# A half-swap copied DRAM to DRAM: engines on neighbouring rows, or each engine on 255 rows of its own

## The chip, the cores and the metric

The kernel runs on one core of a Trainium2 chip. Times are device microseconds for one execution on that core. Transfers are carried out by the core's 16 DMA engines; the SP (SyncE) and ACT (ScalarE) queues issue them, and each has a ring of pending transfers on every one of the 16 engines. In the profile, q1 is the ring set of SP and q10 that of ACT.

## The reference

```python
x = np.random.randn(8192, 8192).astype(np.float32)
def reference(x):
    return np.fft.ifftshift(x)
```

For even sizes this exchanges the halves along both axes: `out[r, c] = x[(r + 4096) % 8192, (c + 4096) % 8192]`. Nothing is computed. 8192 x 8192 floats are 268.44 MB, which have to be read once and written once. A row has 32 KB, and a half row, 4096 floats, 16 KB; in a half row source and destination are both contiguous.

## The kernel before

The copy goes from DRAM to DRAM; no tile in on-chip memory is used, and no engine computes. The loop `for row in range(0, R, ENGINES * per)` makes 16 blocks of 512 output rows. For each block, SP issues one transfer for the left half of the rows (`h = 0`) and ACT one for the right half (`h = hc`), 8 MB each, 32 in all.

A transfer is described by three dimensions, each a step and a count, the outermost first. The outermost one has 16 entries, and entry e is carried out by DMA engine e. The second counts the rows that one engine does for this transfer, the third is the contiguous half row of 4096 floats.

```python
per = 32
dims = [[C, ENGINES], [ENGINES * C, per], [1, hc]]
```

With these steps, engine e does rows `row + e`, `row + e + 16`, `row + e + 32` and so on: at any time the 16 engines are at 16 neighbouring rows, and together they go down the block. The packets that the profile counts are half rows of 16 KB; besides them every engine writes one small completion mark for each transfer.

The order of the work is the order of issue. There are four completion semaphores for SP's transfers and four for ACT's, so the fifth transfer of a queue is issued only when the first has landed, the sixth after the second, and so on. An engine alternates between its ring of q1 and its ring of q10 while both hold work. Line 30 of the code holds the transfers, line 48 the start of the program, line 59 its end.

Of the kernel before, what the change touches and what calls it, by code (L numbers as in the profile page):

```python
# [1 line left out]

# [4 lines left out]


ENGINES = 16


@with_exitstack
def kernel(
    ctx: ExitStack,
    tc: tile.TileContext,
    x: bass.AP,
    out: bass.AP,
):
    nc = tc.nc
    R, C = x.shape  # L20
    hr = R // 2
    hc = C // 2


    per = 32
    dims = [[C, ENGINES], [ENGINES * C, per], [1, hc]]
    for row in range(0, R, ENGINES * per):
        src_row = (row + hr) % R
        for queue, h in ((nc.sync, 0), (nc.scalar, hc)):
            queue.dma_start(  # L30
                out=bass.AP(out.tensor, out.offset + row * C + h, dims),
                in_=bass.AP(x.tensor, x.offset + src_row * C + hc - h, dims),
            )


# [1 line left out]
_INS = ['x']  # L37
_OUTS = [((8192, 8192), 'float32')]


def kernel(**inputs):
    import numpy as _np
    import concourse.bacc as _bacc
    import concourse.tile as _tile
    from concourse import mybir as _mybir
    from concourse.bass_utils import run_bass_kernel_spmd as _run

    nc = _bacc.Bacc("TRN2", target_bir_lowering=False, num_devices=1)  # L48
    arrays, args = {}, []
    for name in _INS:  # L50
        a = _np.ascontiguousarray(inputs[name])
        if a.dtype.kind in "iu":
            a = a.astype(_np.int64)
        arrays[f"in_{name}_dram"] = a
        args.append(nc.dram_tensor(f"in_{name}_dram", a.shape, _mybir.dt.from_np(a.dtype), kind="ExternalInput").ap())
    for i, (shape, dtype) in enumerate(_OUTS):
        dt = _mybir.dt.from_np(_np.dtype(dtype))
        args.append(nc.dram_tensor(f"out_{i}_dram", shape, dt, kind="ExternalOutput").ap())
    with _tile.TileContext(nc) as tc:
        kernel(tc, *args)  # L60
    r = _run(nc, [arrays], core_ids=[0])
    got = tuple(r.results[0][f"out_{i}_dram"] for i in range(len(_OUTS)))
    return got[0]
```

## Time and profile before

| what | value |
|---|---|
| median of 3 runs | 822.56 us (821.65 to 823.45) |
| the profiled execution | 822.98 us, span 821.2 us |
| moved | 268.44 MB read, 268.44 MB written |
| mean rate over the span | 327 GB/s in each direction |
| packets | 16,896: 16,384 of 16 KB and 512 completion marks |
| transfers | 16 from SP, 16 from ACT, 8192 KB each |
| issue to landing | median 204 us, shortest 51.6, longest 207.1 |
| computing engines | 0.2 us busy in all (4 constants written by POOL) |

In the profile the line "DMA" gives the mean busy share of the 16 DMA engines in 40 equal slices of the span, in tenths; the line "GB/s" gives what they moved in each slice, counted once (each byte is read once and written once, so the memory sees twice that). In a table of stretches, the columns behind the times are the busy time of computing engines, the clock of TensorE (unused here), the DMA share, and GB/s. In stretches of a microsecond or two the last two columns are coarse, since a packet is counted whole where it starts.

### The profile page before, as it was taken

How to read it: one execution, taken by the hardware profiler on the slowest of the kernel's cores; microseconds unless marked ns; L12 is line 12 of the kernel's file. 1: busy time of each engine (PE TensorE's matmuls, PEld its weight loads, DVE VectorE, ACT ScalarE, POOL GpSimd, SP SyncE). 2: the span in 40 equal slices, each digit the busy share in tenths (PEclk: the TensorE clock that was granted, in tenths of full speed). 3: DMA queues.
4: the chain of work that ended last, by engine and by line, in shares of the span. 5: the costliest groups of instructions: out<-in, count | busy, mean ns of one | idle time of the engine just before them, and what ended most of it. 6: DMA issues, size and time to landing. Idle time of an engine off the chain costs nothing. (4 is left out here: it accounts for less than half of the span.)

```text
span 821.2 us, 77 instructions
## 1 busy us (share of the span) xinstructions
POOL 0.2 (0%) x4
## 2 busy tenths in 40 slices
POOL 0000000000000000000000000000000000000000
DMA  8999999999999999999999999999999999999998
GB/s 296 333 324 329 331 328 334 330 330 329 327 330 329 331 326 332 332 327 328 330 330 330 330 323 330 324 330 330 332 326 329 330 322 333 329 329 327 330 329 276
DMA packets 16896, 268.44 MB, mean 327 GB/s; under 512 B 512, under 2 KB 512, under 8 KB 512
## 3 DMA queue, kind: packets, MB, share of 16 engines
q1 hardware_dynamic: 8448, 134.22, 50.2%
q10 hardware_dynamic: 8448, 134.22, 49.0%
HBM read 268.44 MB, written 268.44 MB: 654 GB/s over the span
## 5 line engine op out<-in xcount | busy, mean ns | idle before, releaser
L48 POOL MEMSET const-bfloat16-1.0<- 128x1 bf16 x1 | 0.1, 102 | 0.0
L48 POOL MEMSET const-uint8-127<- 128x1 uint8 x1 | 0.1, 102 | 0.0
L48 POOL MEMSET const-float32-0.0<- 128x1 f32 x1 | 0.1, 99 | 0.2 <-issue 0.2
L48 POOL MEMSET const-float32-1.0<- 128x1 f32 x1 | 0.1, 99 | 0.0
## 6 DMA issues: line engine op xcount, KB each, us to landing
out_dram<-in_x_dram ACTq DMA_DIRECT2D x16, 8192.0 KB, 204.1
out_dram<-in_x_dram SPq DMA_DIRECT2D x16, 8192.0 KB, 204.0
```

The source lines that it names most:

```text
L48: nc = _bacc.Bacc("TRN2", target_bir_lowering=False, num_devices=1)
```

## The change

The copy, its half rows and the two queues stay. What changes is which rows an engine does, and in which order. The output is taken in two halves of 4096 rows (`base` 0 and 4096). In a half, engine e owns the 255 rows from `base + 255 * e` on, and goes down them one by one. They are cut into five transfers of 51 rows per engine. 16 x 255 are 4080 rows; the 16 rows left over are one more transfer, with one row per engine. So each queue issues 12 transfers instead of 16, and at one time the engines are at rows that lie 255 rows (8,355,840 B) apart instead of one row (32,768 B).

```diff
-    per = 32
-    dims = [[C, ENGINES], [ENGINES * C, per], [1, hc]]
-    for row in range(0, R, ENGINES * per):
+    pitch = 255
+    parts = [51, 51, 51, 51, 51]
+
+    def copy(queue, h, row, pitch, step, n):
+        dims = [[pitch * C, ENGINES], [step * C, n], [1, hc]]
         src_row = (row + hr) % R
-        for queue, h in ((nc.sync, 0), (nc.scalar, hc)):
-            queue.dma_start(
-                out=bass.AP(out.tensor, out.offset + row * C + h, dims),
-                in_=bass.AP(x.tensor, x.offset + src_row * C + hc - h, dims),
-            )
+        queue.dma_start(
+            out=bass.AP(out.tensor, out.offset + row * C + h, dims),
+            in_=bass.AP(x.tensor, x.offset + src_row * C + hc - h, dims),
+        )
+
+    for base in (0, hr):
+        row = base
+        for n in parts:
+            copy(nc.sync, 0, row, pitch, 1, n)
+            copy(nc.scalar, hc, row, pitch, 1, n)
+            row += n
+        rest = base + ENGINES * pitch
+        if rest < base + hr:
+            copy(nc.sync, 0, rest, 1, 1, 1)
+            copy(nc.scalar, hc, rest, 1, 1, 1)
```

## The prediction

> **What bounds the kernel now.** I read the page from the top: the busy table first, then the slices, the DMA queues, the issues with their landings, then the waits of SP's queue and finally stretches of the span.
>
> ```profile
> span 821.2 us, 77 instructions
> POOL 0.2 (0%) x4
> DMA  8999999999999999999999999999999999999998
> GB/s 296 333 324 329 331 328 334 330 330 329 327 330 329 331 326 332 332 327 328 330 330 330 330 323 330 324 330 330 332 326 329 330 322 333 329 329 327 330 329 276
> DMA packets 16896, 268.44 MB, mean 327 GB/s; under 512 B 512, under 2 KB 512, under 8 KB 512
> q1 hardware_dynamic: 8448, 134.22, 50.2%
> q10 hardware_dynamic: 8448, 134.22, 49.0%
> HBM read 268.44 MB, written 268.44 MB: 654 GB/s over the span
> out_dram<-in_x_dram ACTq DMA_DIRECT2D x16, 8192.0 KB, 204.1
> out_dram<-in_x_dram SPq DMA_DIRECT2D x16, 8192.0 KB, 204.0
> ```
>
> No engine computes. The sixteen DMA engines are occupied from the second slice to the last but one, and the 38 whole slices between lie between 322 and 334 GB/s, mean 329.0. Queues q1 and q10 (SP's and ACT's, equal in bytes) share that time: 50.2 + 49.0%. So the time is bytes over pace, and only the pace can change much.
>
> What sets the pace? The trace has 16,384 packets of 16 KB, one for each half row (the other 512 records are the completion marks). The shortest takes 608 ns, about a third take no more than 611 ns, the median is 733, the mean 795 and the 90th percentile 1,092. An engine can therefore do 16,384 B in 608 ns (16 engines: 431 GB/s), and on average is held up for 187 ns by something outside it. Stretches of the span say more:
>
> ```profile
> core 0: us, POOL busy (x), PEclk, DMA share, GB/s
> 2.00:3.00 1.00, 0.00 (x0) 1.00 1.09 262
> 4.00:5.00 1.00, 0.00 (x0) 1.00 1.02 426
> 5.00:6.00 1.00, 0.00 (x0) 1.00 1.03 393
> 10.00:20.00 10.00, 0.00 (x0) 1.00 0.99 318
> 22.00:412.00 390.00, 0.00 (x0) 1.00 1.00 329
> 412.00:802.00 390.00, 0.00 (x0) 1.00 1.00 329
> ```
>
> The engines do come near their own pace once, at 4 to 6 us; from 6 us on they are held to about 329 GB/s, the same in both halves of the output. In stretches of 50 us the rate stays within 326 to 332 GB/s. If the 187 ns were independent bad luck of each packet (their standard deviation is about a quarter of the mean), 50 us with its thousand packets should scatter by 2.7 GB/s; spread evenly over time, the packets' bytes scatter by 1.0. When one packet is slow, others are fast: the engines share a pool, memory traffic of 2 x 329 = 658 GB/s, and the pool is what is full.
>
> ```profile
> SPq L59 <- DMA out_dram<-in_x_dram: 166.8, 2, 119.1
> SPq L30 <- DMA out_dram<-in_x_dram: 134.4, 12, 51.3
> ```
>
> SP waits for landings, not the engines for SP: an issue lands 204 us later, four blocks of 51 us, so the rings hold work throughout.
>
> **The change part by part.** The profiled execution took 822.98 us, 1.78 over its span, and lies 0.42 above the median of 822.56, so the two can be used as one.
>
> *Bytes and packets.* Two times (5 x 51 x 16 + 16) x 2 queues = 16,384 packets of 16 KB, as before. Nothing gained or lost; each engine keeps 1,024 packets.
>
> *Completion marks.* 24 issues instead of 32, so 384 marks instead of 512, 8 fewer per engine at 9 ns each: -0.07 us.
>
> *Issues.* SP and ACT issue 12 each instead of 16. One takes 0.57 to 0.66 us when there is room in the rings, else it stands some 40 us until there is; either way earlier blocks cover it. Issue i waits for issue i-4 of its queue. The thin cover is around the single-row issue: then two blocks of 51 rows and one row are queued, 103 packets per engine and queue. Two queues alternating at 795 ns make that 164 us of work against an issue of 1 us. Without that cover it would cost about an issue, 0.6 to 1.1 us, each time. I put it at 0.
>
> *Start.* SP's first packet starts 2.19 us into the span, 1.5 us after its issue begins, and ACT's first only 2.95 us after SP's. If the delay grows with rows per issue, SP's first issue becomes 0.65 x 51/32 = 1.04 us, +0.4 us; if not, 0. I take +0.2. ACT's later start costs nothing while q1 alone keeps the engines at 426 GB/s.
>
> *End.* The last landings of an issue are spread over 2.6 to 2.9 us across engines, and the last stretch runs dry in that time. The last issue is now one row instead of 32; the engines' shares of the work are equal before and after. 0, bounds -2.9 (they end together) to +3 (as much more).
>
> *The order of addresses*, the only large term. Before, the sixteen engines read 16 neighbouring rows (512 KB) and write 16 neighbouring rows, and go on together. An engine that falls behind by a few packets still touches row residues (modulo 16) that no other engine touches. After, engine i is at row 255 i + t: sixteen streams 8,355,840 B apart on each side. In step, the residues modulo 16 are again all different, (t - i); but an engine one row behind falls on its neighbour's residue, and the sixteen rows are no more one block. Landings of one issue, spread over 2.6 us near the end against 1.6 us for a row's two packets, say that engines are one to two rows out of step. If memory cares for neighbourhood, the change takes some away; I see nothing that it adds, since an engine's two halves of a row, and the 134 MB between read and write row, stay.
>
> The trace holds no row for such a pattern. Bounds: below, packets at their floor, 268.44 MB / 431 GB/s = 623 us of transfer, 4 us of start and end, 627 us; above, every packet as the 90th percentile, x 1,092/795, 816 us x 1.374 + 7 = about 1,128 us. The nearest row for this kernel with a little less order is its own slowest slices, 322 and 323, mean 322.5 against 329.0: 780 us of whole slices become 780.1 x 329.0/322.5 = 795.8, +15.7 us. I take that.
>
> Sum: 822.98 - 0.07 + 0.2 + 15.7 = 838.8, 839 us.
>
> **A rule weighed.** The measured row is this trace's pitch between engines, 32 KB, with 329 GB/s. The Trainium skill ("DMA: Bandwidth & Descriptors", section "Latency and other measured facts", HBM row pitch at large powers of two) reports that copies with rows 8 MiB apart ran at 103 GB/s per direction, and that 4 KiB of padding on a 4 MiB pitch restored 214. The new pitch is 8 MiB less 32 KiB, so by that rule it counts as padded; unpadded, the sum would be 268.44 MB / 103 GB/s = 2,606 us. Its 214 GB/s is already under what this trace shows, so no run here yet tells what a padded pitch allows at 329. The page "HBM Reference", section "Specifications (TRN2)", gives some 716 GB/s for a domain; by it the copy could not go under 536.9 MB / 716 GB/s = 750 us, an estimate.
>
> **The rivals.**
> - *Only the total counts.* For: the evenness over 50 us, and no difference between the halves of the output. Against: a third of the packets run at the floor and others at twice that, so something finer than a total picks them out. Time: 822.98 + 0.1, 823 us.
> - *Neighbouring rows are the cause of the 187 ns* (the other side). Sixteen streams far apart would then collide less, everywhere in the bulk. For: the start, where only SP's half rows were under way, reached 426 GB/s, so engines and queues leave room. Against: row residues are as distinct before as they can be. Price: by the fastest slices, 334 GB/s, 780.1 x (1 - 329.0/334) = -11.7 us, 811 us; if half of the 187 ns went, 816 x 93/795 = -95 us, 727 us. It decides from 0.3% less held-up time per packet, 2.4 ns of 795.
> - *Sixteen far streams fall on one part of memory.* For: the pitch is within 0.4% of a power of two. Against: the 32 KB step between engines remains. Price: the upper bound, about 1,128 us.
> - *The share of an engine becomes unequal*: an engine with a bad region finishes last and nobody takes over its rows. Before, the last landings of an issue differ by 2.9 us of 816. If one engine ran 3% slower than the mean, +24 us, 847 us; it lies inside the forecast's range.
> - *The change doesn't spread over the engines.* The outer dimension is 16 in all 24 issues, as before, so I give it nothing.
>
> **How the numbers follow.** Slower by some lost order, 825 to 905 us: 0.51. Half a row's collisions or worse, over 905 us (a tenth over now, 75 ns more per packet): 0.10. No difference: 0.11. Faster: 0.28, of which 0.18 is between 800 and 821 and 0.10 below. Leaving out a tenth at each end gives 800 to 905; the likeliest case's own range is 825 to 905. About 0.2% is what a measurement of this kernel can tell from no change (its three runs lie within 0.11% of their median). Slower 0.61, same 0.11, faster 0.28.
>
> **What the profile after would show.** Right: the slices near 322 GB/s, evenly, packets at the floor fewer than a third, landings of one issue spread over more than 2.9 us. The issue terms: 12 issues per queue, none late, no dip in the slices at the single rows (middle of the span). Only the total counts: slices at 329 again. Faster: slices over 334. Unequal engines: the last slices empty slowly. Far streams colliding: slices at 240 or lower. The forecast is wrong if memory gains from long runs of an engine in one region, or doesn't notice.

## The result and the profile after

The changed kernel takes 859.01 us (856.08 to 861.88, 4 runs) where the kernel before took 823.0 us in the runs beside it. The ratio is 1.0445, 95% interval 1.0412 to 1.0477: slower by 36 us. The profiled execution took 859.65 us, its span 857.9.

The page after: the span, the slices, the packets, the queues, the issues.

```profile
span 857.9 us, 69 instructions
...
DMA  9999999999999999999999999999999999999998
GB/s 288 313 311 312 312 316 318 309 322 313 310 310 319 319 312 320 319 312 312 312 319 303 324 319 316 312 312 312 316 319 305 315 316 321 311 315 312 323 312 277
DMA packets 16768, 268.44 MB, mean 313 GB/s; under 512 B 384, under 2 KB 384, under 8 KB 384
## 3 DMA queue, kind: packets, MB, share of 16 engines
q10 hardware_dynamic: 8384, 134.22, 49.6%
q1 hardware_dynamic: 8384, 134.22, 49.4%
HBM read 268.44 MB, written 268.44 MB: 626 GB/s over the span
...
out_dram<-in_x_dram ACTq DMA_DIRECT2D x10, 13056.0 KB, 257.6
out_dram<-in_x_dram SPq DMA_DIRECT2D x10, 13056.0 KB, 257.3
out_dram<-in_x_dram SPq DMA_DIRECT2D x2, 256.0 KB, 230.6
out_dram<-in_x_dram ACTq DMA_DIRECT2D x2, 256.0 KB, 229.6
```

The engines are occupied as before and the bytes are the same; the pace is lower in every slice but the last. The 38 whole slices lie between 303 and 324 GB/s with a mean of 314.6, against 322 to 334 with a mean of 329.0. No slice is empty, and there is no dip at the middle of the span, where the single rows are. In stretches (stretch, its length, POOL, TensorE clock, DMA share, GB/s) both halves of the output look the same, and so does the stretch with the single rows between them:

```profile
22.00:412.00 390.00, 0.00 (x0) 1.00 1.00 314
412.00:425.00 13.00, 0.00 (x0) 1.00 0.98 316
425.00:432.00 7.00, 0.00 (x0) 1.00 0.94 311
432.00:820.00 388.00, 0.00 (x0) 1.00 1.00 315
```

The packets tell where the time went. A 16 KB packet took 795 ns in the mean before and 829.5 ns after; 1,024 packets per engine times 34.4 ns are 35.2 us, nearly all of the 36.7 us between the two profiled executions. The share of packets near the floor (615 ns or less) did not move, 33.0% before and 33.4% after. The slow ones became slower: median 733 to 759 ns, 90th percentile 1,092 to 1,188, 99th 1,421 to 1,564.

### The profile page after: what moved, and what is told of

It reads as the page before. It is cut to its first block, busy times and chain, and to the rows that moved or that the text cites. A ratio compares the mean times of both kernels' runs of the same rounds, so it can differ in the third digit from the quotient of the medians.

```text
span 857.9 us, 69 instructions
## 1 busy us (share of the span) xinstructions
POOL 0.2 (0%) x4
```

## The experiments

All ratios are to the kernel before, run beside the experiment on the same chip. The experiments were run in five sets. In two of them the kernel before took 823 to 824 us, in the other three 813.6 to 814.3; what sets them apart is not shown (the record has the same chip number beside a set of either sort). So ratios are compared from set to set, not times. Distances are in rows of 32 KB, so 256 rows are 8,388,608 B and 64 rows 2,097,152 B. "Short of" 256 rows means the pitch between engines is that much less. The residue of a row modulo 16 is what is left when its number is divided by 16. Two engines coincide when their rows lie a multiple of 64 rows apart (or of 128 or 256). Three theories were carried along. A: the loss goes by the extent over which the sixteen streams lie. B: going row by row costs, because an engine out of step falls on the residue modulo 16 rows of its neighbour (the prediction's own idea). C: a pitch near a multiple of a large power of two costs, because engines a row out of step, or the traffic they leave behind, coincide.

**Issues alone.** The old order of rows in the new issues:

```diff
-            copy(nc.sync, 0, row, pitch, 1, n)
+            copy(nc.sync, 0, base + 816 * part, 1, 16, 51)   # ACT alike
```

> The rows of the kernel before (16 neighbouring rows, each engine 16 rows on), in the issues of the kernel after (51 rows per engine, and one row at the end of each half). If the issues cost nothing and the order of addresses is the whole loss: 823 us, ratio 1.00 within 0.3%. If the new issues carry the loss (late starts, the thin cover at the single row): 850 us or more.

822.43 us, ratio 0.9989 (0.9971 to 1.0007). The issues, the single rows and their thin cover cost nothing that can be measured: the order of addresses is the whole loss.

**51 rows apart.** Going down row by row in the issues of the kernel after:

```diff
-    pitch = 255
+    pitch = 51            # five blocks of 816 rows instead of one of 4080
```

> The kernel after in issues and in going down row by row, with the engines 51 rows apart instead of 255. Theory A, the streams lie too far apart and the loss grows with the distance: between the two, some 830 to 850 us. Theory B, going row by row is what costs, since an engine out of step falls on the residue (modulo 16 rows) of its neighbour, whatever the distance: 859 us as with 255. Theory C, the single pitch of 255 rows is an unlucky one: 823 us.

822.46 us, ratio 0.9998 (0.9982 to 1.0014). Nothing is lost. But it is not shown that each engine walked a region of its own here. Sixteen regions of 51 rows that adjoin are one run of 816 rows, and in the trace the transfer names them so: `dst_num_elem=[816,1]`, where the kernel after has `[51,16]`. Which engine did which of the 816 rows is not recorded. The landings of one issue are spread over 2.1 us in the median, as in the old order in the same issues (2.3 us); with 61 and 115 rows below, whose transfers keep their 16 entries, it is 1.0 and 1.3 us, in the kernel after 1.8. So this run decides nothing between the theories. Theory B falls by 61 and 115 rows: there too an engine one row out of step falls on the residue modulo 16 of another, and 0.6 and 0.2% are lost.

**A walk that keeps the residues, far apart:**

```diff
-            copy(nc.sync, 0, row, 255, 1, 51)
+            copy(nc.sync, 0, base + c, 241, 16, 15)   # c = 0 to 15
```

> Engines 241 rows apart, each going on 16 rows at a time, so that each keeps a residue of its own (modulo 16 rows) whatever the engines are out of step; the rows left over are done as in the kernel before (6% of the rows). Theory B (lost residues): back to 823 to 826 us. Theory A (distance): 855 to 860 us. If it is clearly slower than 859, then an engine's own walk over neighbouring rows was worth something and was saving time in the kernel after.

Four runs took 837.98 to 840.48 us, a fifth 854.45; the ratio of the four is 1.0200 (1.0173 to 1.0226). Neither of the two numbers expected: less than half of the loss stays, but not none.

**Exactly 256 rows apart:**

```diff
-    pitch = 255
+    pitch = 256           # 51, 51, 51, 51, 51 and 1 rows, none left over
```

> The kernel after with 256 rows (8,388,608 B) between engines, no rows left over. All engines in step have the same residue. If residues matter in this pattern (theory B, and the Trainium skill's row on HBM row pitch at large powers of two, in DMA: Bandwidth & Descriptors, which would give 103 GB/s per direction and some 2,600 us): far slower, over 1,100 us. If only distance counts (theory A): 859 us.

Four runs took 1,784.83 to 2,172.92 us (median 1,846.86), 2.2 to 2.6 times the time before. The slices of the fastest, of the page:

```profile
GB/s 144 156 151 158 150 154 148 149 153 151 151 151 152 154 150 149 148 156 151 148 150 157 150 152 151 150 149 147 152 145 155 156 151 150 146 151 147 154 150 136
```

One row more between engines than in the changed kernel, and the pace is halved. So how engines stand to one another counts for far more than anything the trace of before showed, and 255 is next to a cliff. The Trainium skill's row on HBM row pitch at large powers of two ("DMA: Bandwidth & Descriptors", "Latency and other measured facts") gives 103 GB/s per direction for rows 8 MiB apart. This run agrees that the rate falls, and measures 151 GB/s.

**127 and 239 rows apart:**

```diff
-    pitch = 255
+    pitch = 127           # and, in another kernel, 239
```

> Engines 127 rows apart, row by row, in two blocks per half of the output; 32 rows left over as in the kernel before. What is known: 51 rows apart costs nothing, 255 apart 4.4%. Theory A (the loss grows with the extent that the sixteen streams span, 27 MB at 51 rows, 67 MB here, 134 MB at 255): between, 830 to 845 us. Theory C (the loss comes from near coincidence: a pitch of 256 rows takes 1,847 us, and with 255 an engine one row out of step comes exactly onto such a multiple of its neighbour): 127 is one row short of half that pitch, so two engines apart coincide when two rows out of step: some loss, 825 to 845 us, so this run alone doesn't tell them apart, but with 239 it does.

> Engines 239 rows apart, row by row, 17 rows short of 256: no engine comes onto a multiple of 256 rows of its neighbour unless it is 17 rows out of step; 272 of 4096 rows are left over and done as in the kernel before. Theory A (extent, 125 MB): 854 to 858 us. Theory C (near coincidence): 823 us. Between the two, both are at work.

127 rows: 841.51 us, ratio 1.0335 (1.0293 to 1.0377). 239 rows: 834.75 us, ratio 1.0254 (1.0211 to 1.0298). Extent alone falls: the wider pitch loses less. But coincidence alone does not hold either: 239 should have been free.

**Only the reads, or only the writes, 255 rows apart:**

```diff
+    FAR, NEAR = (255, 1, 51), (1, ENGINES, 51 * ENGINES)
...
+            copy(nc.sync, 0, base, part, 51, NEAR, FAR)     # out NEAR, in FAR; in another kernel FAR, NEAR
```

> Only the reads are 255 rows apart and row by row; the writes go to 16 neighbouring rows as in the kernel before, so rows land in other places than the reference has them (the same bytes are read and written). If the loss of 36 us is on the read side: 859 us; if on the write side: 823 us; if shared, some 841 us. Theory A allows any split; theory C, where reads and writes each collide among themselves, expects a split too.

> Only the writes are 255 rows apart and row by row; the reads come from 16 neighbouring rows as in the kernel before, so rows land in other places than the reference has them. The complement of the run with far reads: 859 us if writes carry the loss, 823 if reads do, 841 if they share it. If both mixed runs are at 859 or above, it isn't the one side or the other but that reads and writes no longer keep a fixed distance of 4096 rows.

Far reads: 831.9 us, ratio 1.0224 (1.0175 to 1.0273). Far writes: 817.53 us, ratio 1.0036 (1.0004 to 1.0067). The reads carry most of it. The two together give 2.6%, less than the 4.2 to 4.5 of the full change; these kernels also give up the fixed distance between read row and write row, and 255 itself was not run in that set, so I don't read more from the difference.

**255 again, and 251, 205 and 63 rows apart, all in one set:**

```diff
-    pitch = 255
+    pitch = 251           # 205, 63 in other kernels; rows left over as in the kernel before
```

> The kernel after once more, as the measure for its neighbours on the same chip: ratio 1.0445 to the kernel before, as measured; the chip of the runs with 127 and 239 rows was 1% faster for the kernel before, and this says whether the loss is the same on it.

> Engines 251 rows apart, 5 short of 256, more than the one or two rows that engines were seen out of step; 80 of 4096 rows left over, done as in the kernel before. Known: 239 apart costs 2.5%, 255 apart 4.4%. Theory C (the extra 1.9% of 255 is engines one or two rows out of step that come onto a multiple of 256 rows): 2.5 to 2.7%, as with 239. Theory A (extent alone): 4.3%, as with 255.

> Engines 205 rows apart, extent 107 MB, far from 256 and 128; a fifth of the rows (the last 51 per engine of each half) is left over and done as in the kernel before, so the far part and the near part can be compared inside one trace. Theory A (extent): in the far part a loss of about 3 to 3.5%, in the whole 2.4 to 2.8%. Theory C (coincidence alone): no loss, 0 to 0.3%.

> Engines 63 rows apart, one short of 64 rows (2,097,152 B), extent 33 MB, close to the 27 MB of the pitch of 51 that cost nothing. Theory A (extent): 0 to 0.6%. Theory C, if multiples of 64 rows are already a coincidence: 1% or more; the Trainium skill's row on HBM row pitch at large powers of two (DMA: Bandwidth & Descriptors) lists a pitch of 2 MiB at 164 GB/s against 207 at 512 KiB and 103 at 8 MiB, so a weaker one than at 8 MiB.

| pitch | short of a power of two by | extent of 16 streams | us | ratio (interval) |
|---|---|---|---|---|
| 255 | 1 row (256) | 134 MB | 859.14 | 1.0422 (1.0390 to 1.0454) |
| 251 | 5 rows (256) | 132 MB | 832.45 | 1.0106 (1.0079 to 1.0133) |
| 205 | 51 rows (256) | 107 MB | 835.29 | 1.0136 (1.0106 to 1.0165) |
| 63 | 1 row (64) | 33 MB | 847.63 | 1.0286 (1.0261 to 1.0310) |

Four rows less pitch give back 26.7 of the 35.3 us, over practically the same extent. And 63 rows, one short of 64, lose 2.9%, where 61 rows, over practically the same extent, lose 0.6% (below). For the greater part that is what theory C expects of neighbouring engines. Something is left at 251 and 205. In the trace of 205 the far part of each half (20 to 320 and 435 to 735 us) can be compared with the rows left over, done in the old order:

```profile
20.00:320.00 300.00, 0.00 (x0) 1.00 1.00 322
345.00:410.00 65.00, 0.00 (x0) 1.00 0.99 328
435.00:735.00 300.00, 0.00 (x0) 1.00 1.00 321
760.00:820.00 60.00, 0.00 (x0) 1.00 1.00 330
```

321 and 322 against 328 and 330 GB/s: in the far part 2 to 3%.

**The same pitch of 255 with a walk that cannot coincide:**

```diff
-            copy(nc.sync, 0, row, 255, 1, 51)
+            copy(nc.sync, 0, base + c, 255, 16, 15)   # c = 0 to 15
+            # then 15 rows per engine row by row, and the 16 left over
```

> The pitch of the kernel after, 255 rows, but each engine goes on 16 rows at a time through its region, so that engines out of step by any number of rows never come onto a multiple of 256 rows of one another (the last 15 rows of each region are still done row by row). Theory C (the greater part of the 36 us is engines one or two rows out of step that coincide): the loss falls from 4.2% to the 1 to 2% that 241 rows with this walk, 251 and 205 rows show, 832 to 840 us. If 255 is a bad pitch for another reason, whatever the walk: 4.2%, 858 us.

824.61 us, ratio 1.0131 (1.0093 to 1.0169), where 255 row by row had 1.0422 and 1.0445. The trace holds its own control. The columns are as above; the short stretches are those of the last 15 rows of each region, which go row by row:

```profile
20.00:380.00 360.00, 0.00 (x0) 1.00 1.00 329
386.00:408.00 22.00, 0.00 (x0) 1.00 1.01 319
425.00:785.00 360.00, 0.00 (x0) 1.00 0.99 330
793.00:814.00 21.00, 0.00 (x0) 1.00 0.98 319
```

In one execution, with the same regions and the same pitch, 16 rows at a time gives 329 and 330 GB/s, row by row 319, twice. It does not give everything back: in the same set, the old order runs at 334 and 335 GB/s (the rows left over in the run with 179 rows, below).

**61 and 64 rows apart, around 63:**

```diff
-    pitch = 63
+    pitch = 61            # and, in another kernel, 64
```

> Engines 61 rows apart, 3 short of 64, extent 32 MB as with 63 (2.9% slower). 192 of 4096 rows are left over, done as in the kernel before. Theory C: three rows is more than the engines are out of step, so the loss falls to below 1%. Without coincidence, at this extent, whatever made 63 slow stays: 2.7%.

> Engines exactly 64 rows (2,097,152 B) apart, no rows left over. Theory C needs a coincidence at 64 rows to be costly by itself, since 63 is to suffer from it only part of the time: at least 15% slower, 950 us or more. If it is 3% or less, multiples of 64 rows aren't what hurts 63.

61 rows: 819.28 us, ratio 1.0061 (1.0038 to 1.0084). 64 rows: four runs of 1,256.90 to 1,284.00 us; the two lower ones give the ratio 1.5476 (1.5384 to 1.5567). In the page of 64 rows the slices are low and uneven:

```profile
GB/s 209 218 207 219 206 224 220 199 231 209 216 218 199 222 209 214 219 195 220 208 214 223 194 228 213 213 227 192 219 214 215 227 199 221 219 202 228 199 218 190
```

So 64 rows cost 55%, one row less 2.9%, three rows less 0.6%.

**What remains: 51's standing over a wider extent.** 179 = 128 + 51 and 115 = 64 + 51; and 51 once more in a set of the faster sort:

```diff
-    pitch = 51
+    pitch = 179           # 115 in another kernel
```

> Engines 179 rows apart: modulo 128 rows the sixteen engines stand just as with 51 rows (179 = 128 + 51), which cost nothing, but over 94 MB instead of 27. 30% of the rows, at the end of each half, are done as in the kernel before. Theory A for what remains of the loss without coincidences (extent): the first part at 322 to 325 GB/s against 328 to 330 in the second, 0.8 to 1.6% in the whole. If only the standing modulo 128 rows counts: no difference between the parts, 0 to 0.2%.

> Engines 115 = 64 + 51 rows apart: modulo 64 rows they stand as with 51, over 60 MB; 416 of 4096 rows are done as in the kernel before. If what remains of the loss grows with the extent: between 51 rows (27 MB) and 179 rows (94 MB, its far part 2.3% slower than its near part), 0.7 to 1.5% in the whole. If it doesn't go by extent but by how the engines stand modulo 128 rows or more, anything from 0 to 3%.

> The pitch of 51 rows once more, beside 115 on one chip, since the chips differ by 1% in the kernel before and the far pitches were measured on both sorts. If 51 rows cost nothing: ratio 0.997 to 1.003 again. If the loss-free result belonged to the one chip alone: 1.005 or more on a chip where the kernel before takes 813 us.

179 rows: 822.18 us, ratio 1.0091 (1.0061 to 1.0122). 115 rows: 816.22 us, ratio 1.0023 (1.0007 to 1.0038). 51 rows: 812.46 us, ratio 0.9988 (0.9963 to 1.0013). In the trace of 179, the far part (first and third stretch) beside the old order:

```profile
20.00:270.00 250.00, 0.00 (x0) 1.00 0.99 327
300.00:400.00 100.00, 0.00 (x0) 1.00 1.00 334
430.00:680.00 250.00, 0.00 (x0) 1.00 1.00 325
710.00:805.00 95.00, 0.00 (x0) 1.00 1.00 335
```

The loss grows from 115 to 179 with the same standing modulo 64 rows, so extent, or address bits above 64 rows, count for something. The run with 51 rows can't be put before them in this row, since its transfers again name 816 rows in one list. But 115 lost less than expected, and the other pitches don't line up by extent (239: 2.5%, 241 with the fixed walk: 2.0, 205: 1.4, 255 with the fixed walk: 1.3, 251: 1.1, 61: 0.6).

The pitches were chosen by the distance of neighbouring engines. Engines five apart are 575 rows apart with 115 (one short of 9 x 64), 895 with 179 (one short of 7 x 128) and 1,025 with 205 (one past 4 x 256). Those are eleven pairs of engines, beside the fifteen pairs of neighbours that stand so with 63, 127 and 255. So part of what 179 and 205 lose can be coincidence too, and these runs don't tell it from extent. On the other side, 115 loses far less than eleven pairs against fifteen would give, or 18 against 42 that stand within three rows (0.2% against 2.9% with 63), and 239, where only the first and the last engine come so close (3,585 rows, one past 14 x 256), loses 2.5%. A count of such pairs alone does not fit all runs. What the remainder of 0.2 to 2.5% depends on stays open.

## Why the prediction was right and wrong

*Direction and place: right.* The time went where the order of addresses was put, and all of it: the old order in the new issues takes 0.9989 of the time.

*Issues, marks, start, end: right.* Put at -0.07, 0, +0.2 and 0 us. SP's first issue took 0.69 us instead of the 1.04 that a growth with rows would give; its first packet started 2.22 us into the span, against 2.19. The last landings are spread over 2.3 to 2.6 us, against 2.6 to 2.9. The price of an issue was read a little low: ACT's second and third issue took 0.90 and 0.88 us before, not 0.57 to 0.66.

*The size of the address term: wrong, and this is the step that failed.* I took +15.7 us, "its own slowest slices, 322 and 323", as the price of a little less order; it measured about 36 us (859.01 against 823.0), of which the packets show 35.2. A kernel's slowest slice is chance within the one order that it has, and holds nothing of another order. The upper bound of 1,128 us from the 90th percentile was not safe either: 256 rows, one row further, takes 1,785 or more. The time itself lay inside the range, 800 to 905. (Of the range's own working, 82 us up to 905 are 80 ns more per packet, not 75; and start and end enter the lower bound with 4 us and the upper with 7. Neither changes the forecast.)

*The mechanism: half right.* The prediction said that an engine one row behind "falls on its neighbour's residue". That a pitch one row short is hurt, and that a walk which cannot coincide gives back most of the loss, the runs show (1.0422 against 1.0131, and 319 against 329 GB/s in one trace). But the residue is not the one modulo 16 rows that the prediction named: 61 and 115 rows walk across those residues too and lose 0.6 and 0.2%. The largest losses short of the cliff, 2.9, 3.4 and 4.2%, came where neighbouring engines stood one row short of 64, 128 and 256. The prediction had that in its third rival ("the pitch is within 0.4% of a power of two"), priced it at the upper bound, and held against it that "the 32 KB step between engines remains". That step takes away nearly all of the cliff (from 2.2 times or more to 1.04), but not the last 4%. That engines out of step are the link is argued and not shown. It rests on distance, 1 row costing and 3 or 5 rows much less; no record shows which engine was where, traffic of a neighbour still under way one row behind would look the same, and the pairs five engines apart don't fit it.

*Out of step more than before: wrong.* I expected landings of one issue spread over more than 2.9 us; they are spread over 0.9 to 2.6. The sign could not have told anything, since the kernel before already reaches 3.3 us (1.2 to 3.3 over its 32 issues). With 1.66 us for two packets in a row, 0.9 to 2.6 us are between half a row and one row and a half, enough for a pitch one row short.

*Fewer packets at the floor: wrong.* The share is the same (33.0 and 33.4%); the tail grew. Packets above the floor took longer, and most so the slowest (99th percentile 1,421 to 1,564 ns).

*The rule weighed: right in kind.* By the Trainium skill's row, 8 MiB less 32 KiB "counts as padded". The runs show that 32 KiB less bring 151 GB/s up to about 314, and 160 KiB less (251 rows) to about 325, where the old order has 329. No run here has the page's padding of 4 KiB.

*The rivals.* "Only the total counts" is excluded by 256 and 64 rows, although the slices of the changed kernel are nearly as even as before: evenness over 50 us did not mean that the addresses don't matter. "Neighbouring rows are the cause of the 187 ns" is not borne out: in none of these runs did other distances between engines make the copy measurably faster; the best far one, 115 rows, is 0.2% slower. Unequal engines: all of them land within 2.6 us.

## What to carry to other kernels

Where many engines walk through memory side by side, work out the distance between neighbouring engines, also for one or two steps out of step, and keep it off multiples of large powers of two by several rows, not by one: one row short of 256 still cost 4.2% here and five rows short 1.1%, one row short of 64 cost 2.9% and three rows short 0.6%. That alone does not make a wide order free: 239 rows lost 2.5%, so measure the pitch that you take. Look also at what the trace says a transfer became: dimensions that adjoin can be written as one list, and then the code no longer says which engine does which rows. A trace with one order of addresses does not price another; set the range from kernels that had the other order, and weigh a cliff that is one step away by more than all or nothing. A kernel that does a part of its rows in another order carries its own control, since the two parts can be compared inside one execution.

## What the runs showed of the hardware that was not expected

- The cliff is steep on both scales: 64 rows (2,097,152 B) between engines take 1.55 times the time, 256 rows 2.2 times or more; one row less, 1.029 and 1.042.
- Reads suffer more than writes from the far order: 2.2% against 0.4%.
- Sixteen engines that each walk a region of their own need not lose against 16 neighbouring rows: 115 rows apart cost 0.2%, over an extent of 60 MB.
- The same kernel differs by 1% from one set of runs to another (823 to 824 against 813.6 to 814.3 us).
